# A hand-written attention schedule: a pair's loads and splits, the inverse rows and the branch fill moved to other slots

## The chip, the cores and the metric

One core of a Trainium2 chip runs the whole program. The metric is the device time of one execution in microseconds (us), the median of several runs. TensorE (PE) does the matmuls; VectorE (DVE) and ScalarE (ACT) read its results from PSUM; GpSimd (POOL) adds the mask; SyncE (SP) issues nearly all loads. Each of them takes its own instructions in the order of the program.

## The reference

One layer of an encoder, over 1024 positions of width 1024, all in float32:

```python
h = rmsnorm(x, norm_mix_pre)
m = mixer(h, w_in, b_f, conv_w, w_branch, w_out)
x = x + rmsnorm(m, norm_mix_post)
h = rmsnorm(x, norm_ffn_pre)
x = x + rmsnorm(swiglu(h, w_gate_up, w_down), norm_ffn_post)
```

The mixer has two branches. A is a gated short convolution, `ya`. B is causal softmax attention of 8 heads of width 64, whose logits carry a bias from cumulated forget gates, `yb`. They meet in

```python
merged = sigmoid(gate_conv) * (ya @ w_branch[0]) + sigmoid(gate_attn) * (yb @ w_branch[1])
return merged @ w_out
```

## The kernel before

Every product of two float32 operands is made of three: each operand is split into a rounded high part (a copy on ACT) and the rest (a subtraction on VectorE), and `mm3` multiplies high by high, high by low and low by high. The kernel projects q, k, v, the gates and the convolution's inputs, runs the attention, then the product with `w_branch[1]` (tile `pbb`), `w_out`, and the feed-forward part. The change touches the attention only, some 180 us of the span.

**Steps and slots.** Heads go in pairs `j` = 0 to 3 (the two heads are `e` = 0, 1), queries in blocks `i` of 128. A step (j, i) handles one query block of one pair against its (i + 1) * 128 keys. `steps` (line 697) lists the 32 steps: pairs 0 to 2 go from i = 7 down to 0, pair 3 goes 3, 2, 1, 0, 7, 6, 5, 4. A step is *wide* where its scores need over 512 columns. The loop at line 1008 runs slots t = 2 to 33; steps 0 and 1 are begun inside the projection before it (`last_pair`). In slot t stand, in this order of the program:

- `step_qk(t)`: the scores of step t, tiles `sp`. A wide step takes both score banks, a narrow one takes one; a bank is free again when the row maxima that read it are done.
- `pv_pair(t - 2)`: the products of the weights of step t - 2 with v, tile `po`, drained into `yb` on ACT every fourth step.
- `turn_bank(t - 1, ...)`: the exponentials of step t - 1 are transposed on PE (tiles `tps`, two banks) and copied to `ptT`, partly on ACT and partly on VectorE.
- `row_max(t, e)` on VectorE (a custom operation that adds the bias row `cb`, writes `pt` and leaves the negated maximum `nm`), then `expo(t, e)` on ACT, which also sums the rows into `rsum`.
- `mask_of(t + 1)` on POOL.
- `units[t]` units of *branch fill*: a unit is three matmuls (one k of an `mm3`) of `ya @ w_branch[0]`, tile `pba`, in bank `mb`. Four units make a half of one of eight column blocks `d`; then VectorE multiplies it by the gate into `um`. On PE the units stand between the transpositions of the two heads.
- whatever the table `at[t]` (lines 980 to 1006) lists for the slot.

The table's entries are `load_pair(j)` (bias rows `cb`, q and k, v), `split_q` and `split_k` (the quarter splits of q into `hi` and `lo`, and of k, whose low half is subtracted in place: tile `lo` or `kl`), `load_ya` and `split_ya` (`yh`, `yl`), `load_wa`, `split_wa` (`s`, `s4h`, `s4l`) and `load_sg` (gates), `load_wb` and `split_wb`, and the inverse rows: `invert(j)` takes the reciprocals `ri` of the row sums on VectorE, transposes them on PE (`tr`, in a `tps` bank), copies `tr` to `rT` on VectorE, stores that to memory (`ri_dram`) and loads it back spread over the partitions (`rb`). `divide(j, n)` multiplies half n of `yb` by `rb`.

Since the instructions of the attention are kept in the program's order (`strict`), an engine that waits holds back all that stands behind it in its queue. SyncE has nothing but loads and stores to do, and issues each as soon as its buffer and its data allow, often ahead of the slot that lists it.

**Where things stand.** Before the change `load_pair(j + 1)` is listed in slot 8j + 4, its splits in 8j + 5 to 8j + 7, so the last one, with the subtraction of the low half of k, right ahead of the pair's first slot 8j + 8. `invert(j)` stands at the end of slot 8j + 9, a wide step. Pair 3 is inverted in two halves, at the end of slot 29 and behind the loop. The fill covers d = 0 to 5 and ends in slot 31. Behind the loop `load_wa(7)` is issued, and four halves of branch products (d = 6, 7) run on the banks of `psm2`, beside the splits of `wb` and `yb`; then come the `pbb` products. All recorded instructions have line 73, that of a helper, so they are told apart by tiles.

Of the kernel before, what the change touches and what calls it, by code (L numbers as in the profile page):

```python
# [10 lines left out]
F32 = mybir.dt.float32  # L11
# [6 lines left out]
P = 128  # L18
S = 1024
D = 1024  # L20
KT = D // P
ST = S // P
NC = 512
H = 8
HD = 64
# [20 lines left out]
def block_kernel(  # L46
# [18 lines left out]
    class InOrder:  # L65
# [46 lines left out]
    def mul(o, a, b):  # L112
        nc.vector.tensor_tensor(o, a, b, op=ALU.mult)
# [53 lines left out]
    def st_tile(name, w=1):  # L167
        return stat.tile([P, w], F32, tag=name, name=name)
# [470 lines left out]
    def row_max(t, e):  # L639

        j, i = steps[t]
        n = (i + 1) * P
        sp, b = sps[t][e]
        cb = cb_of(j, e, j == 3 and i > 3)
        pt, nm = p_tile(t, e), st_tile("nm")
        if n <= NC:
            args = pt[:, :n], sp[:, b, :n], cb[:, :n]
        else:
            args = (
                pt[:, :n].rearrange("p (b k) -> p b k", b=2),  # L650
                sp[:, :, : n // 2],
                cb[:, :n].rearrange("p (b k) -> p b k", b=2),
            )
# [214 lines left out]
    def load_wa(d):  # L868
        was[d] = s4_t()
        nc.sync.dma_start(  # L870
            was[d], w_branch[0, 0][:, d * P : (d + 1) * P].rearrange("(k p) m -> p k m", p=P)
        )

    def load_sg(d):
        for n, ns in enumerate((n1, n2)):
            sgs[d, n] = sg_tile()
            nc.sync.dma_start(sgs[d, n], sg_dram[d][0][:, ns])

    def split_wa(d):
        wh, wl = s4h_t(), s4l_t()  # L880
        split(wh, wl, was[d])
        was[d] = wh, wl

    def branch_a(d, n, psp, tag):

        ns = (n1, n2)[n]
        ps = psp.tile([P, NC], F32, tag=tag, name="pba")
        wh, wl = was[d]
        for k in range(4):
            mm3(  # L890
                ps, (wh[:, k, :], wl[:, k, :]), (ya2[n][0][:, k, :], ya2[n][1][:, k, :]),
                k == 0, k == 3,
            )
            yield None if k < 3 else lambda: mul(um[:, d, ns], sgs[d, n], ps)

    FILL = 6

    def filler():
        for d in range(FILL):
            for n in range(2):  # L900
                yield from branch_a(d, n, pst, "mb")

    def inverse_rows(j, half=None):

        rs = rsums[j].rearrange("p (e i) -> p e i", e=2)
        if half is not None:
            rs = rs[:, :, 4 * half : 4 * half + 4]
        w = rs.shape[-1]
        ri = st_tile("ri", 2 * ST)[:, : 2 * w].rearrange("p (e i) -> p e i", e=2)
        nc.vector.reciprocal(ri, rs)  # L910
        tr = pss.tile([P, 4, P], F32, tag="T", name="tr", bufs=2)[: 2 * w, 0, :]
        nc.tensor.transpose(tr, ri.rearrange("p e i -> p (e i)"), ident)
        rT = t1.tile([2 * ST, P], F32, tag="rT", name="rT", bufs=2)[: 2 * w, :]
        nc.vector.tensor_copy(rT, tr)
        to = slice(0, S) if half is None else (n1, n2)[half]
        for e in range(2):
            nc.sync.dma_start(
                ri_dram[j][e][to].rearrange("(i p) -> i p", p=P), rT[e * w : (e + 1) * w, :]
            )
        rb = tp_.tile([P, S], F32, tag="rb", name="rb", bufs=1)[:, : w * P]  # L920
        for e in range(2):
            nc.sync.dma_start(
                rb[e * HD : (e + 1) * HD, :], ri_dram[j][e][to].partition_broadcast(HD)
            )
        return rb
# [22 lines left out]
    def divide(j, n, half=None):  # L948
        ns = (n1, n2)[n]
        mul(yb[:, j, ns], yb[:, j, ns], rbs[j][:, ns if half is None else n1])  # L950

    fill = filler()
    units = {t: 1 for t in (9, 10, *range(16, 20), *range(28, 32))}
    for t in (12, 20, 24):
        units |= {t - 1 if t == 12 else t: 2, t: 2, t + 1: 2, t + 2: 4, t + 3: 4}
    rbs, wbr = {}, {}
    wbh, wbl = [], []

    def invert(j, half=None):
        rbs[j] = inverse_rows(j, half)  # L960

    def load_pair(j):
        cb_of(j, 0)
# [13 lines left out]
    def do(f, *args):  # L977
        return lambda: f(*args)

    at = defaultdict(list)  # L980
    for j in range(3):
        o = 8 * j
        at[o + 4].append(do(load_pair, j + 1))
        at[o + 5] += [do(qk_tiles, j + 1), do(split_q, j + 1, n1)]
        at[o + 6] += [do(split_q, j + 1, n2), do(split_k, j + 1, n1)]
        at[o + 7].append(do(split_k, j + 1, n2))
        at[o + 9].append(do(invert, j))
        for n in range(2):
            at[o + 12 + n].append(do(divide, j, n))
    at[29].append(do(invert, 3, 0))  # L990
    at[32].append(do(divide, 3, 0, 0))
    at[25] += [do(cb_of, 3, 0, True), do(cb_of, 3, 1, True)]
    for t, n, m in ((2, 0, 0), (5, 0, 2), (9, 1, 0), (11, 1, 2)):
        at[t].append(do(load_ya, n, m))
    for t, n, m in (
        (3, 0, 0), (4, 0, 1), (7, 0, 2), (8, 0, 3), (10, 1, 0), (11, 1, 1), (12, 1, 2), (12, 1, 3),
    ):
        at[t].append(do(split_ya, n, m))
    for d, t in enumerate((5, 10, 13, 16, 21, 24, 26)):
        at[t] += [do(load_wa, d), do(load_sg, d)]  # L1000
    for d, t in enumerate((8, 11, 15, 19, 22, 25, 28)):
        at[t].append(do(split_wa, d))
    for k in range(4):
        at[26].append(do(load_wb, k))
# [1 line left out]
        at[t].append(do(split_wb, k))  # L1006

    for t in range(2, NU + 2):
        if t < NU:
            step_qk(t)  # L1010
        pv_pair(t - 2)
        back = t - 1 if t <= NU else None
        wide = back and steps[back][1] > 5
        if back:
            da = turn_bank(back, 0, 0, "ACT")
            db = turn_bank(back, 0, 1, "DVE")
            da()
        if t < NU:
            row_max(t, 0)
        if back and db:  # L1020
            db()
        if t < NU:
            expo(t, 0)
        muls = [m for m in (next(fill, None) for _ in range(units.get(t, 0))) if m]
        if back:
            dc = turn_bank(back, 1, 0, "ACT" if wide else "DVE")
            dd = turn_bank(back, 1, 1, "DVE" if wide else "ACT")
        if t < NU:
            row_max(t, 1)
# [12 lines left out]
    assert not at, at  # L1042
    invert(3, 1)
    for unit in fill:
        if unit:
            unit()
    pss_close()
    pst_close()

# [4 lines left out]
    def yb_split(n, ks):  # L1054
        ns = (n1, n2)[n]
        for k in ks:
            split(yb2[n][0][:, k, :], yb2[n][1][:, k, :], yb[:, k, ns])

    load_wa(KT - 1)
    for m in branch_a(KT - 2, 0, psm, "mm"):  # L1060
        pass
    m()
    split_wa(KT - 1)
    load_sg(KT - 1)
    split_wb(2)
    for m in branch_a(KT - 1, 0, psm, "mm"):
        pass
# [8 lines left out]
    m()  # L1076
    for m in branch_a(KT - 1, 1, psm, "mm"):
        pass
    yb_split(0, (2, 3))
    m()  # L1080
    divide(3, 1, 1)
    yb2.append(halves_of(1))
    yb_split(1, range(4))
    strict[0] = False
# [447 lines left out]
```

## Time and profile before

| what | value |
|---|---|
| median of 3 runs | 1395.58 us (1395.28 to 1396.58) |
| the profiled execution | 1396.29 us |
| its span, first to last instruction | 1394.5 us |
| PE busy | 1351.4 us (97%) |
| VectorE busy | 935.6 us (67%) |
| ACT busy | 536.4 us (38%) |
| mean granted clock of PE | 0.991 |

A row of the timeline gives the start in us from the span's start, the duration in us, engine, line, operation, `out<-in`, the shapes, the count, and in brackets the engine's idle time before it with what ended it. A row of the sums by stretch gives the stretch, its length, then for PE, PE's weight loads, VectorE, ACT and POOL the busy time with the number of instructions, the granted PE clock (1.00 is full, 0.50 half), and the DMA share with GB/s. Matmuls overlap in the records, so a row of 0.39 us may start 0.23 us after the one before. Slot t begins with its first `sp` row; slot 8 is at 445.06, slot 16 at 491.23, slot 24 at 533.63.

### The profile page before, as it was taken

How to read it: one execution, taken by the hardware profiler on the slowest of the kernel's cores; microseconds unless marked ns; L12 is line 12 of the kernel's file. 1: busy time of each engine (PE TensorE's matmuls, PEld its weight loads, DVE VectorE, ACT ScalarE, POOL GpSimd, SP SyncE). 2: the span in 40 equal slices, each digit the busy share in tenths (PEclk: the TensorE clock that was granted, in tenths of full speed). 3: DMA queues.
4: the chain of work that ended last, by engine and by line, in shares of the span. 5: the costliest groups of instructions: out<-in, count | busy, mean ns of one | idle time of the engine just before them, and what ended most of it. 6: DMA issues, size and time to landing. Idle time of an engine off the chain costs nothing.

```text
span 1394.5 us, 17740 instructions
## 1 busy us (share of the span) xinstructions
PE 1351.4 (97%) x6726; PEld 1102.9 (79%) x6726; DVE 935.6 (67%) x1451; ACT 536.4 (38%) x853; POOL 127.5 (9%) x256
## 2 busy tenths in 40 slices
PE   7999999999998999799999999999999999999997
PEld 7978888888876776688887778888888888888886
DVE  6873767655546654584678699767776676776585
ACT  6541222233345653442446432222232223444452
POOL 0001000011112111000001121111100111000000
PEclk9999999999999999999999999999999999999999
DMA  6332422333314543353234556332332325975541
GB/s 213 106 99 83 137 65 87 114 98 121 106 64 141 167 129 113 130 183 120 91 102 139 161 183 186 98 114 99 113 97 100 113 99 181 353 273 188 173 159 61
DMA packets 153558, 186.88 MB, mean 134 GB/s; under 512 B 9456, under 2 KB 106800, under 8 KB 153472
## 3 DMA queue, kind: packets, MB, share of 16 engines
q1 hardware_dynamic: 138736, 137.19, 31.4%
q0 software_dynamic: 14736, 48.54, 9.4%
q8 instruction: 53, 0.87, 0.2%
q14 instruction: 33, 0.27, 0.1%
HBM read 136.62 MB, written 49.09 MB: 133 GB/s over the span
## 4 chain that ended last, share of the span: by engine, by line
PE 54%; DVE 3%; issue 2%; ACT 1%; DMA 1%; POOL 0%; SPq 0%; DVEq 0%; POOLq 0%; ACTq 0%
PE b L73 27%; PE pd L73 15%; PE pm L73 5%; PE pbb L73 3%; PE pba L73 2%; PE po L73 1%; PE sp L73 0%; DVE tt L73 0%; PE tps L73 0%; PE tp L73 0%; DMA pre_dram<-c 0%; ACT tt L73 0%; ACT pt L73 0%; DVE ptT L73 0%; DMA raw<-in_w_gate_up_dram 0%
## 5 line engine op out<-in xcount | busy, mean ns | idle before, releaser
L73 DVE TENSOR_TENSOR c<-c,b 128x512 f32<-128x512 f32 x195 | 133.1, 683 | 95.8 <-PE b L73 76.8
L73 DVE TENSOR_TENSOR lo<-raw,hi 128x1024 fp32r<-128x1024 f32 (+1 forms) x93 | 112.1, 1205 | 86.0 <-PE b L73 71.4
L73 ACT ACTIVATE hi<-raw 128x1024 fp32r<-128x1024 f32 (+1 forms) x100 | 101.8, 1018 | 130.8 <-PE b L73 76.7
L73 PE MATMUL b<-hth,hi 128*128 128x512 f32 x352 | 139.0, 395 | 0.0
L73 PE MATMUL b<-hth,lo 128*128 128x512 f32 x352 | 138.1, 392 | 0.0
L73 PE MATMUL b<-htl,hi 128*128 128x512 f32 x352 | 137.2, 390 | 0.0
L73 ACT ACTIVATE hi<-sx 128x1024 fp32r<-128x1024 f32 x41 | 43.5, 1061 | 223.1 <-PE b L73 197.5
L73 PEld LDWEIGHTS b<-hth,lo 128*128 128x128 f32 x352 | 66.0, 188 | 15.6
L73 PEld LDWEIGHTS b<-hth,hi 128*128 128x128 f32 x352 | 66.1, 188 | 14.6 <-DVE c L73 0.8
L73 PEld LDWEIGHTS b<-htl,hi 128*128 128x128 f32 x352 | 66.1, 188 | 14.6
L73 DVE TENSOR_TENSOR lo<-sx,hi 128x1024 fp32r<-128x1024 f32 x41 | 50.2, 1224 | 34.4 <-PE b L73 30.8
L73 PE MATMUL b<-hah,hi 128*128 128x512 f32 x176 | 70.4, 403 | 1.9 <-ACT c L73 1.9
L73 PE MATMUL b<-hah,lo 128*128 128x512 f32 x176 | 69.5, 396 | 0.0
L73 PE MATMUL b<-hal,hi 128*128 128x512 f32 x176 | 69.3, 394 | 0.0
L73 DVE TENSOR_TENSOR sx<-raw 128x512 f32<-128x512 f32 x78 | 53.7, 688 | 20.4 <-DMA raw<-in_w_in_dram 10.8
L73 PE MATMUL pd<-hi,lo 128*128 128x512 f32 x160 | 62.6, 391 | 0.0
L73 PE MATMUL pd<-hi 128*128 128x512 f32 x160 | 62.3, 392 | 0.0
L73 PE MATMUL pd<-glo,ghi 128*128 128x512 f32 x148 | 57.7, 390 | 0.0
L73 PE MATMUL pd<-ghi 128*128 128x512 f32 x148 | 57.6, 390 | 0.0
L73 PE MATMUL pd<-ghi,glo 128*128 128x512 f32 x148 | 57.6, 389 | 0.0
L73 PE MATMUL b<-hT34h,lo 128*128 128x512 f32 x136 | 53.4, 393 | 0.0
L73 PE MATMUL b<-hT12h,lo 128*128 128x512 f32 x136 | 53.4, 393 | 0.0
(364 smaller groups left out, 3401.2 us busy)
## 6 DMA issues: line engine op xcount, KB each, us to landing
raw<-in_w_gate_up_dram SPq DMA_DIRECT2D x51, 512.0 KB, 3.7
raw<-in_w_in_dram SPq DMA_DIRECT2D x35, 512.0 KB, 4.5
a_dramS<-um POOLq DMA_DIRECT2D x44, 256.0 KB, 2.8
a_dramA<-um POOLq DMA_DIRECT2D x33, 256.0 KB, 2.8
xt<-in_x_dram SPq DMA_DIRECT2D x16, 512.0 KB, 3.5
sg<-sg_dram SPq DMA_DIRECT2D x32, 256.0 KB, 4.3
graw<-a_dramS SPq DMA_DIRECT2D x14, 512.0 KB
sg_dram<-c POOLq DMA_DIRECT2D x24, 256.0 KB, 2.3
```

The costliest lines, as they stand in the source:

```text
L73: ins = getattr(self.engine, name)(*args, **kw)
```

## The change

It rewrites the slot table and three pieces of code around it.

- `load_pair(j + 1)` moves from slot 8j + 4 to 8j + 2, the quarter splits from 8j + 5 to 7 to 8j + 4 to 6. The loads and splits of `ya`, of the branch weights and of the gates get new slots; d = 7 is now loaded and split inside the loop.
- The inverse is cut in two. `inverse(j)`, the reciprocal, stands at the end of slot 8j + 10. `inverse_rows` stands in slot 8j + 12, a narrow step (for pair 2 that is slot 28, a wide one): the transposition right behind the scores, in the branch bank `mb`, and `rT` behind the slot's first row maximum. The divisions move two slots on. Pair 3 is inverted once, not in halves, at the end of slot 32 and in slot 33.
- The fill begins in slot 8, covers 13 halves instead of 12 (d = 6, n = 0 is the new one), and has units in slots 32 and 33.
- In slots 2 to 7 the first head's transpositions stand ahead of `pv_pair`, not behind it.

The core of the diff:

```diff
-        at[o + 4].append(do(load_pair, j + 1))
-        at[o + 5] += [do(qk_tiles, j + 1), do(split_q, j + 1, n1)]
-        at[o + 6] += [do(split_q, j + 1, n2), do(split_k, j + 1, n1)]
-        at[o + 7].append(do(split_k, j + 1, n2))
-        at[o + 9].append(do(invert, j))
+        at[o + 2].append(do(load_pair, j + 1))
+        at[o + 4] += [do(qk_tiles, j + 1), do(split_q, j + 1, n1)]
+        at[o + 5] += [do(split_q, j + 1, n2), do(split_k, j + 1, n1)]
+        at[o + 6].append(do(split_k, j + 1, n2))
+        at[o + 10].append(do(inverse, j))
+        rows[o + 12] = j
         for n in range(2):
-            at[o + 12 + n].append(do(divide, j, n))
-    at[29].append(do(invert, 3, 0))
-    at[32].append(do(divide, 3, 0, 0))
+            at[o + 14 + n].append(do(divide, j, n))
+    at[32].append(do(inverse, 3))
...
-    for d, t in enumerate((8, 11, 15, 19, 22, 25, 28)):
+    for d, t in enumerate((7, 11, 15, 18, 22, 25, 28, 32)):
         at[t].append(do(split_wa, d))
...
     for t in range(2, NU + 2):
+        turned = None
         if t < NU:
             step_qk(t)
-        pv_pair(t - 2)
+        if t in rows:
+            turned = inverse_rows(rows[t], pst, "mb")
+        if t == NU + 1:
+            turned = inverse_rows(3, pss, "T", 2)
...
+        if t >= 8:
+            pv_pair(t - 2)
         if back:
             da = turn_bank(back, 0, 0, "ACT")
             db = turn_bank(back, 0, 1, "DVE")
             da()
+        if t < 8:
+            pv_pair(t - 2)
         if t < NU:
             row_max(t, 0)
+        if turned:
+            turned()
...
-    invert(3, 1)
-    for unit in fill:
-        if unit:
-            unit()
...
-    load_wa(KT - 1)
-    for m in branch_a(KT - 2, 0, psm, "mm"):
-        pass
-    m()
-    split_wa(KT - 1)
-    load_sg(KT - 1)
...
+    divide(3, 0)
     yb_split(0, (2, 3))
     m()
-    divide(3, 1, 1)
+    divide(3, 1)
```

In the new `units` the slots 8 to 15 have 1, 1, 1, 1, 2, 2, 4, 4 units (before, from slot 9: 1, 1, 2, 2, 2, 4, 4), slots 16 to 31 what they had, slots 32 and 33 two each.

VectorE, from the last drain of slot 6 to the first row maximum of slot 8 (`ISA pt,nm` is a row maximum, `ISA nm` its read-out). Before:

```order
L73 COPY ptT<-tps 128x384
L73 SCALAR_TENSOR_TENSOR lo<-raw,hi 128x512
L73 ISA pt,nm<-sp,cb 128x128
L73 ISA nm 128x1
L73 ISA pt,nm<-sp,cb 128x128
L73 ISA nm 128x1
L73 COPY ptT<-tps 128x256
L73 TENSOR_TENSOR lo<-lo,hi 128x1024
L73 TENSOR_TENSOR yl_3476<-raw,yh_3475 128x512
L73 ISA pt,nm<-sp,cb 128x1024
```

and now:

```order
L73 COPY ptT<-tps 128x384
L73 TENSOR_TENSOR lo<-lo,hi 128x1024
L73 TENSOR_TENSOR yl_3476<-raw,yh_3475 128x512
L73 ISA pt,nm<-sp,cb 128x128
L73 ISA nm 128x1
L73 ISA pt,nm<-sp,cb 128x128
L73 ISA nm 128x1
L73 COPY ptT<-tps 128x256
L73 TENSOR_TENSOR yl_3476<-raw,yh_3475 128x512
L73 TENSOR_TENSOR s4l<-s_3684,s4h 128x512
L73 ISA pt,nm<-sp,cb 128x1024
```

The subtraction of the low half of k (`lo<-lo,hi`) and a `yl` have moved ahead of slot 7's two row maxima; another `yl` and the weight split `s4l` now stand behind them.

PE, at the inverse rows of pair 0. Before, `tr` is the first matmul behind slot 9's transpositions, ahead of slot 10's scores:

```order
L73 MATMUL tps<-ident,pt 128x128 x8
L73 MATMUL tr<-ident,ri 16x128
L73 MATMUL sp<-hi 128x384 x2
L73 MATMUL sp<-lo,hi 128x384 x2
L73 MATMUL sp<-hi,lo 128x384 x2
```

Now it stands in slot 12, between the scores and the value products:

```order
L73 MATMUL sp<-hi 128x512 x2
L73 MATMUL sp<-lo,hi 128x512 x2
L73 MATMUL sp<-hi,lo 128x512 x2
L73 MATMUL tr<-ident,ri 16x128
L73 MATMUL po<-ptT,v 64x128 x12
L73 MATMUL tps<-ident,pt 128x128 x5
```

It has moved from behind a pair of transpositions to behind a step's scores, with the value products queued behind it.

PE, slots 32 and 33. Before:

```order
L73 MATMUL po<-ptT,v 64x128 x12
L73 MATMUL tps<-ident,pt 128x128 x10
L73 MATMUL po<-ptT,v 64x128 x10
L73 MATMUL tr<-ident,ri 8x128
L73 MATMUL pba<-yh_3475,s4h 128x512
```

and now:

```order
L73 MATMUL po<-ptT,v 64x128 x12
L73 MATMUL tps<-ident,pt 128x128 x5
L73 MATMUL pba<-yh_3475,s4h 128x512
L73 MATMUL pba<-yl_3476,s4h 128x512
L73 MATMUL pba<-yh_3475,s4l 128x512
L73 MATMUL pba<-yh_3475,s4h 128x512
L73 MATMUL pba<-yl_3476,s4h 128x512
L73 MATMUL pba<-yh_3475,s4l 128x512
L73 MATMUL tps<-ident,pt 128x128 x5
L73 MATMUL tr<-ident,ri 16x128
L73 MATMUL po<-ptT,v 64x128 x10
L73 MATMUL pba<-yh_3475,s4h 128x512
```

Six branch products have come between the two heads' transpositions, and `tr` stands ahead of the last value products.

More of the change, by code (lines that the diff above doesn't have):

```diff
@@ L894, in branch_a, with inverse, inverse_rows, drain @@
             yield None if k < 3 else lambda: mul(um[:, d, ns], sgs[d, n], ps)
-    FILL = 6
+    FILL = 2 * 6 + 1
     def filler():
[L899 to L925, printed above, removed]
+        for h in range(FILL):
+            yield from branch_a(h // 2, h % 2, pst, "mb")
+    invs, rbs = {}, {}
+    def inverse(j):
+        invs[j] = st_tile("ri", 2 * ST)
+        nc.vector.reciprocal(invs[j], rsums[j])
+    def inverse_rows(j, psp, tag, bufs=1):
+        tr = psp.tile([P, 4, P], F32, tag=tag, name="tr", bufs=bufs)[: 2 * ST, 0, :]
+        nc.tensor.transpose(tr, invs[j], ident)
+        def drain():
+            rT = t1.tile([2 * ST, P], F32, tag="rT", name="rT", bufs=2)
+            nc.vector.tensor_copy(rT, tr)
+            for e in range(2):
+                nc.sync.dma_start(
+                    ri_dram[j][e].rearrange("(i p) -> i p", p=P), rT[e * ST : (e + 1) * ST, :]
+                )
+            rb = rbs[j] = tp_.tile([P, S], F32, tag="rb", name="rb", bufs=1)
+            for e in range(2):
+                nc.sync.dma_start(
+                    rb[e * HD : (e + 1) * HD, :], ri_dram[j][e].partition_broadcast(HD)
+                )
+        return drain
     po = [None]
@@ L946, in pv_pair, with divide @@
             )
-    def divide(j, n, half=None):
+    def divide(j, n):
         ns = (n1, n2)[n]
-        mul(yb[:, j, ns], yb[:, j, ns], rbs[j][:, ns if half is None else n1])
+        mul(yb[:, j, ns], yb[:, j, ns], rbs[j][:, ns])
     fill = filler()
[L953 to L956, printed above, removed]
+    units = {}
+    for t in range(8, 32, 8):
+        if t < 24:
+            units |= {t: 1, t + 1: 1, t + 2: 1, t + 3: 1, t + 4: 2, t + 5: 2, t + 6: 4, t + 7: 4}
+        else:
+            units |= {t: 2, t + 1: 2, t + 2: 4, t + 3: 4, t + 4: 1, t + 5: 1, t + 6: 1, t + 7: 1}
+    units |= {32: 2, 33: 2}
+    wbr = {}
     wbh, wbl = [], []
-    def invert(j, half=None):
-        rbs[j] = inverse_rows(j, half)
     def load_pair(j):
@@ L978, in do @@
         return lambda: f(*args)
-    at = defaultdict(list)
+    at, rows = defaultdict(list), {}
+    at[2].append(do(load_ya, 0, 0))
     for j in range(3):
         o = 8 * j
-        at[o + 4].append(do(load_pair, j + 1))
-        at[o + 5] += [do(qk_tiles, j + 1), do(split_q, j + 1, n1)]
-        at[o + 6] += [do(split_q, j + 1, n2), do(split_k, j + 1, n1)]
-        at[o + 7].append(do(split_k, j + 1, n2))
-        at[o + 9].append(do(invert, j))
+        at[o + 2].append(do(load_pair, j + 1))
[4 more added lines that the diff above has]
+        rows[o + 12] = j
         for n in range(2):
-            at[o + 12 + n].append(do(divide, j, n))
-    at[29].append(do(invert, 3, 0))
-    at[32].append(do(divide, 3, 0, 0))
+            at[o + 14 + n].append(do(divide, j, n))
+    at[32].append(do(inverse, 3))
     at[25] += [do(cb_of, 3, 0, True), do(cb_of, 3, 1, True)]
-    for t, n, m in ((2, 0, 0), (5, 0, 2), (9, 1, 0), (11, 1, 2)):
+    for t, n, m in ((3, 0, 2), (3, 1, 0), (6, 1, 2)):
         at[t].append(do(load_ya, n, m))
     for t, n, m in (
-        (3, 0, 0), (4, 0, 1), (7, 0, 2), (8, 0, 3), (10, 1, 0), (11, 1, 1), (12, 1, 2), (12, 1, 3),
+        (3, 0, 0), (4, 0, 1), (6, 0, 2), (7, 0, 3), (8, 1, 0), (9, 1, 1), (10, 1, 2), (11, 1, 3),
     ):
         at[t].append(do(split_ya, n, m))
-    for d, t in enumerate((5, 10, 13, 16, 21, 24, 26)):
-        at[t] += [do(load_wa, d), do(load_sg, d)]
-    for d, t in enumerate((8, 11, 15, 19, 22, 25, 28)):
+    for d, t in enumerate((4, 8, 12, 15, 19, 23, 26, 29)):
+        at[t].append(do(load_wa, d))
+    for d, t in enumerate((4, 8, 14, 16, 22, 24, 27, 32)):
+        at[t].append(do(load_sg, d))
+    for d, t in enumerate((7, 11, 15, 18, 22, 25, 28, 32)):
         at[t].append(do(split_wa, d))
@@ L1041, in block_kernel @@
             f()
-    assert not at, at
-    invert(3, 1)
-    for unit in fill:
-        if unit:
-            unit()
+    assert not at and next(fill, None) is None, at
     pss_close()
```

## The prediction

> **What bounds the kernel now.** The page first. TensorE (PE) is busy nearly all the span:
>
> ```profile
> PE 1351.4 (97%) x6726; PEld 1102.9 (79%) x6726; DVE 935.6 (67%) x1451; ACT 536.4 (38%) x853; POOL 127.5 (9%) x256
> ```
>
> The profiled execution took 1396.29 us, 0.71 over the median 1395.58; the sum below is a difference, and I take it off the median. An edit that moves work can only win PE's waits or its clock. So the view of waits comes second, for PE alone between 420 and 620 us, the stretch of the attention loop:
>
> ```profile
> PE tr L73 <- DVE ri L73: 5.7, 4, 1.8
> PE sp L73 <- DVE lo L73: 3.9, 2, 2.0
> PE pba L73 <- ACT s4h L73: 3.3, 1, 3.3
> PE sp L73 <- DVE kl L73: 1.8, 1, 1.8
> PE sp L73 <- DVE nm L73: 1.7, 3, 0.6
> PE tps L73 <- DVE ptT L73: 1.6, 3, 0.7
> PE po L73 <- DVE ptT L73: 1.1, 3, 0.4
> PE tps L73 <- ACT ptT L73: 0.8, 2, 0.5
> PE pba L73 <- ACT yb L73: 0.5, 1, 0.5
> ```
>
> Columns: us in total, times, longest. Together 20.4 us. The third view is the sums by stretch, whose column before the last two is the granted clock. Four stretches hold half-clock time: slot 8 (445.06), slot 24 (533.63), slot 30 (567.03) and the branch products behind the loop (586.20). The others are slots 11, 16, 18, 19 and 26, for comparison:
>
> ```profile
> 445.06:452.04 6.98, 4.80 (x23) 2.72 (x22) 4.08 (x11) 2.22 (x7) 0.04 (x1) 0.76 0.01 4
> 465.76:471.47 5.71, 5.71 (x59) 4.87 (x59) 2.97 (x8) 3.34 (x7) 0.92 (x2) 1.00 0.96 312
> 491.23:496.56 5.33, 3.51 (x26) 2.16 (x26) 4.21 (x7) 0.41 (x2) 0.14 (x1) 1.00 0.23 69
> 503.26:508.78 5.52, 5.52 (x63) 4.74 (x62) 2.60 (x6) 1.75 (x6) 0.46 (x1) 1.00 0.48 119
> 508.78:513.88 5.10, 5.10 (x56) 4.26 (x55) 2.74 (x9) 2.69 (x6) 0.97 (x3) 1.00 0.99 314
> 533.63:540.38 6.75, 4.93 (x24) 3.06 (x23) 3.47 (x7) 1.68 (x5) 0.92 (x2) 0.76 0.19 66
> 545.87:551.05 5.18, 5.18 (x41) 4.13 (x41) 1.57 (x6) 1.47 (x5) 0.87 (x2) 1.00 0.51 112
> 567.03:574.15 7.12, 7.12 (x62) 6.14 (x61) 3.77 (x7) 2.14 (x5) 0.45 (x1) 0.76 0.51 148
> 586.20:604.00 17.80, 14.51 (x49) 11.26 (x50) 7.55 (x11) 7.19 (x11) 0.00 (x0) 0.81 0.41 132
> ```
>
> So waits and clock together offer about 28 us, and no edit here can win more.
>
> **1. Loads and quarter splits.** The loads gain nothing by themselves: SyncE runs ahead of the slots as buffers come free, and pair 1's rows, placed in slot 4, were issued at slot 2's end:
>
> ```profile
> 425.99 0.91 SPq L73 DMA_DIRECT2D cb<-c_dram x2
> 446.94 1.23 DVE L73 TENSOR_TENSOR lo<-lo,hi 128x1024 fp32r<-128x1024 f32 x1 [0.98 <-ACT hi L73]
> 448.08 0.68 DVE L73 TENSOR_TENSOR yl<-raw,yh 128x512 fp32r<-128x512 f32 x1
> 444.52 0.69 DVE L73 SCALAR_TENSOR_TENSOR lo<-raw,hi 128x512 fp32r<-128x512 f32 x1 [0.93 <-ACT hi L73]
> ```
>
> The splits do. The next pair's scores stop for the low half of k (`lo`, `kl`): 2.0, 1.9 and 1.8 us. One slot earlier that subtraction is over before slots 16 and 24 ask, under 12 branch products each in slots 14, 15, 22 and 23. In slot 16 a division and the weight split, about 0.7 each, still stand ahead of the row maximum; I give 0.3 back there: 1.5 and 1.8. The first pair has no branch fill above it. There 1.23 + 0.68 now stand on VectorE before slot 7's row maxima in place of 0.69, so those end 1.1 to 1.2 later, and they free the bank that slot 8's second head needs. Against 2.0 lost I expect 1.6 again: 0.4. Sum 3.7; bounds 2.5 (first gone wholly, second 1.0) to 5.5.
>
> **2. Half clock.** Cost: one minus the granted clock, times the stretch: 0.24 x 6.98 = 1.7 (slot 8, of which PE would in part have waited for row maxima: 1.1), 0.24 x 6.75 = 1.6 (slot 24, 1.45 with the wait in it), 0.19 x 17.8 = 3.4 (behind the loop, 2.8 while it had work). Slot 30 against slot 18, which does the same work at full clock: 7.12 - 5.52 = 1.6, of which 0.5 returns, as row maximum and copies are then last. Each stretch follows a PE wait of 1.7 us or more, and those waits go. Sum 6.4; bounds 3.0 (two stretches return) to 7.4. [...]
>
> **3. Inverse rows.** Before, PE's transposition of the reciprocals (`tr`) stands first in a slot, behind copy and reciprocal:
>
> ```profile
> 460.01 0.27 PE L73 MATMUL tr<-ident,ri 128*16 128x128 f32 x1 [1.20 <-DVE ri L73]
> 503.06 0.27 PE L73 MATMUL tr<-ident,ri 128*16 128x128 f32 x1 [1.07 <-DVE ri L73]
> 545.67 0.27 PE L73 MATMUL tr<-ident,ri 128*16 128x128 f32 x1 [1.63 <-DVE ri L73]
> 566.83 0.27 PE L73 MATMUL tr<-ident,ri 128*8 128x128 f32 x1 [1.75 <-DVE ri L73]
> 459.01 0.08 DVE L73 DVE_READ_ACCUMULATOR2_ANT nm<- 128x1 f32 x1
> 502.07 0.08 DVE L73 DVE_READ_ACCUMULATOR2_ANT nm<- 128x1 f32 x1
> 565.29 0.08 DVE L73 DVE_READ_ACCUMULATOR2_ANT nm<- 128x1 f32 x1
> 503.26 0.44 PE L73 MATMUL sp<-hi 64*128 64x384 f32 x2
> ```
>
> The scores follow 0.20 after (503.26 - 503.06). Without `tr` three of the four sites still wait for the second row maximum, read out at 459.09, 502.15 and 565.37. They start earlier by 460.21 - 459.09 = 1.1, 1.1 and 567.03 - 565.37 = 1.65; the narrow one, at 545.67, by 1.63 + 0.20 = 1.8. Sum 5.65.
>
> The new place costs. In slots 12 and 20 `tr` writes the branch bank, so PE waits for the product just finished to be drained, with the value products (`po`) queued behind:
>
> ```profile
> 472.15 0.68 DVE L73 TENSOR_TENSOR um<-sg,pba 128x512 f32<-128x512 f32 x1
> 472.37 1.53 PE L73 MATMUL po<-ptT,v 128*64 128x128 f32 x24
> 474.59 0.68 DVE L73 CUSTOM_DVE_ANT_0 pt<-sp,cb 128x512 f32<-128x512 f32 x1
> ```
>
> `um` ends at 472.83, `po` stood ready at 472.37: 0.5 and 0.2 for `tr`, twice 0.7. In slot 12 the next branch product must also wait until `rT` is copied, behind the row maximum at 474.59: 0.4 more. In slot 28 the row maxima are last anyway: 0.2. Net 5.65 - 2.0 = 3.6; bounds 2.0 to 5.2.
>
> **4. Slots 2 to 7.** `po` now stands between the two heads' transpositions and covers their drains:
>
> ```profile
> 436.00 0.74 PE L73 MATMUL tps<-ident,pt 128*128 128x128 f32 x5 [0.48 <-DVE ptT L73]
> 443.64 0.87 PE L73 MATMUL po<-ptT,v 128*64 128x128 f32 x10 [0.30 <-DVE ptT L73]
> ```
>
> With the 0.8 on ACT's `ptT` that is 1.6. In slots 5 to 7 the first head's transposition comes before its exponential is ready; I give 0.7 back: 0.9; bounds 0 to 1.6.
>
> **5. Slot 32 and the tail.** Two units of branch fill stand in slot 32 between the transpositions, two in slot 33, and d = 7's weights are loaded and split inside the loop.
>
> ```profile
> 582.82 0.74 PE L73 MATMUL tps<-ident,pt 128*128 128x128 f32 x5 [0.48 <-DVE ptT L73]
> 584.23 1.31 PE L73 MATMUL po<-ptT,v 128*64 128x128 f32 x18 [0.31 <-DVE ptT L73]
> 588.43 0.58 SPq L73 DMA_DIRECT2D s<-in_w_branch_dram x1
> 591.85 0.63 ACT L73 ACTIVATE s4h<-s 128x512 fp32r<-128x512 f32 x1 [5.68 <-DMA s<-in_w_branch_dram]
> ```
>
> Gone: 3.3 (`s4h`), 0.5 (`yb`), 0.5 and 0.3. New: `tr` of the last pair stands before `po`, behind copy and reciprocal as at 503.06, so about 0.95 + 0.2. The last pair's whole division now comes behind a round trip through memory, but 42 branch products lie above it, 8.5 us at the 0.2 apiece that three more of them make in slot 11 than in slot 19 (5.71 - 5.10). Net 3.4; bounds 2.0 to 4.5. Products and DMAs keep their number but for one transposition, two `ri` stores and two `rb` loads; POOL's masks stay.
>
> **6. One unit from slot 11 to slot 8.** Slot 8 waits for row maxima anyway; slot 11 falls from 5.71 to slot 19's 5.10: 0.6; bounds 0 to 0.6.
>
> Sum: 3.7 + 6.4 + 3.6 + 0.9 + 3.4 + 0.6 = 18.6. 1395.6 - 18.6 = 1377.0.
>
> **The rivals.** *Waits that move.* VectorE and ACT work their queues in order, so the earlier splits hold back row maxima in slots 7 to 10, PE's new waits again pass 1.7 us, and half clock returns there and in one later slot. Then terms 1 and 2 stand at their lower ends (2.5 and 3.0), 3 and 4 lose 1.5: 18.6 - 1.2 - 3.4 - 1.5 = 12.5, so 1383. For it: the 1.6 of part 1 lies close to the 1.7. *The clock does not follow these waits.* In slot 16 a wait of 1.8, and before slot 26 one of 1.63, left the clock at 1.00, so the windows could fall where they will: term 2 is 0, 1383.4. [...] Against it: four of four half-clock stretches stand right behind such waits. *Nothing moves.* The loads already ran ahead, and if row maxima are last wherever a wait goes, 1395. Against it: PE's transpositions end long before the row maxima only at the wide steps. *Branch weights arrive late: slower.* ACT stops in order for them. At 591.85 it stood 5.7 us, and PE 3.3, with 3.4 from issue (588.43) to use. If each of seven loads inside the loop brought such a stop, 7 x 3.3 = 23 us against 18.6: 1400. It decides once a load lands over one slot late; against it, the table gives each two to three slots of some 5 us.
>
> **How the numbers follow.** Forecast 0.66; moved waits 0.17; clock 0.05; nothing 0.03; late weights 0.04; better than all my terms but within the 28 us 0.05. Lower end: the upper bounds, 5.5 + 7.4 + 5.2 + 1.6 + 4.5 + 0.6 = 24.8, give 1371. Upper end: the lower bounds, 2.5 + 3.0 + 2.0 + 0 + 2.0 + 0 = 9.5, would give 1386; that they meet is unlikely, and 1384.5 takes in both rivals near 1383. About 0.15 lies outside. By 0.2% (2.8 us, about what a measurement of this kernel can tell from no change): faster 0.93, same 0.03, slower 0.04.
>
> **What would show it.** Right: no PE wait on `lo`, `kl`, `s4h` or, at slots 9, 17, 25 and 29, on `ri`; one wait on `ri` near 1 us before the last `po`; waits on `nm` in their place of 0.1 to 0.6; a wait of `tr` on `um` near 0.5 twice; granted clock 1.00 in slots 24 and 30 and in the tail; the stretch from slot 2 to the first `pbb` some 18 us shorter. Wrong: half clock in two or more stretches, waits over 1 us on `nm` or `ptT` in slots 7 to 10, ACT stopped for `in_w_branch`, or a wait in the `pbb` products for the last division.

## The result, and the profile after

The changed kernel takes 1373.8 us (1373.32 to 1374.06, 4 runs) against 1395.43 for the kernel before on the same chip: a ratio of 0.9847, 95% interval 0.983 to 0.9864. It is 21.6 us faster; 18.6 were forecast. The profiled execution took 1373.6 us, with a span of 1371.8. PE's row of the page, and PE's waits between 420 and 620 us (us in total, times, longest):

```profile
PE 1341.8 (98%) x6725; PEld 1096.7 (80%) x6725; DVE 933.8 (68%) x1449; ACT 536.1 (39%) x853; POOL 127.9 (9%) x256
```

```profile
PE sp L73 <- DVE nm L73: 3.3, 5, 1.2
PE pba L73 <- DVE rT L73: 1.1, 2, 0.7
PE tps L73 <- ACT pt L73: 1.0, 2, 0.6
PE tr L73 <- ACT s4h L73: 0.9, 1, 0.9
PE tr L73 <- DVE um L73: 0.5, 2, 0.3
PE po L73 <- DVE ptT L73: 0.4, 1, 0.4
PE tps L73 <- DVE ptT L73: 0.2, 1, 0.2
```

The waits on `lo`, `kl`, `ri` and `s4h` that stood at the head of the list are gone, 20.4 us have become 7.4. (The row that names `s4h` is the last pair's `tr`, which waits for its reciprocal. In the variant below that has no weight split there, a_tail_back, the same wait of 0.9 stands as `tr <- DVE ri`.) The sums by stretch place the gain: a stretch runs from one slot's first scores to another's, the last one to the first `pbb`. Of the kernel before, as far as the prediction has not shown them:

```profile
421.85:445.06 23.21, 21.60 (x236) 17.05 (x235) 13.74 (x33) 15.72 (x38) 5.90 (x13) 1.00 0.59 204
452.04:460.21 8.17, 5.61 (x38) 3.73 (x38) 5.90 (x12) 7.17 (x14) 1.78 (x4) 1.00 0.00 0
460.21:491.23 31.02, 31.02 (x280) 25.23 (x280) 18.54 (x45) 18.62 (x46) 5.37 (x12) 1.00 0.57 188
496.56:503.26 6.70, 5.12 (x37) 3.78 (x36) 4.68 (x10) 5.98 (x11) 1.68 (x4) 1.00 0.18 62
503.26:533.63 30.37, 30.37 (x278) 24.57 (x278) 16.86 (x42) 16.27 (x42) 5.38 (x12) 1.00 0.47 143
540.38:545.87 5.49, 3.86 (x26) 2.78 (x25) 2.78 (x8) 2.91 (x7) 0.93 (x2) 0.98 0.00 0
545.87:559.20 13.33, 13.33 (x101) 10.17 (x100) 5.50 (x17) 2.97 (x12) 1.82 (x5) 1.00 0.80 255
559.20:567.03 7.83, 5.33 (x37) 3.74 (x36) 6.75 (x13) 7.20 (x13) 1.79 (x4) 1.00 0.35 140
574.15:603.77 29.62, 24.64 (x160) 19.19 (x159) 14.37 (x26) 13.57 (x23) 0.46 (x1) 0.88 0.32 106
```

and of the changed one:

```profile
422.27:444.14 21.87, 20.91 (x235) 16.42 (x234) 14.12 (x34) 16.73 (x40) 5.92 (x13) 1.00 0.76 265
444.14:449.65 5.51, 3.82 (x26) 2.34 (x26) 4.53 (x12) 2.41 (x8) 0.00 (x0) 1.00 0.03 7
449.65:455.57 5.92, 5.08 (x35) 3.67 (x35) 4.24 (x8) 5.25 (x10) 1.37 (x3) 1.00 0.93 244
455.57:487.58 32.01, 31.35 (x279) 24.88 (x278) 19.69 (x48) 19.20 (x46) 5.87 (x13) 1.00 0.33 104
487.58:491.11 3.53, 3.31 (x27) 2.16 (x26) 3.42 (x7) 0.28 (x1) 0.00 (x0) 1.00 0.02 5
491.11:496.63 5.52, 4.84 (x35) 3.67 (x35) 3.85 (x7) 4.82 (x9) 1.37 (x3) 1.00 0.77 217
496.63:527.83 31.20, 30.93 (x278) 24.84 (x277) 18.40 (x46) 17.45 (x43) 5.88 (x13) 1.00 0.35 116
527.83:531.07 3.24, 3.24 (x23) 2.15 (x22) 2.84 (x7) 1.08 (x4) 0.67 (x2) 1.00 0.75 234
531.07:534.58 3.51, 3.51 (x25) 2.61 (x25) 1.34 (x5) 2.98 (x9) 1.17 (x3) 1.00 0.74 297
534.58:549.32 14.74, 14.07 (x101) 10.49 (x100) 7.74 (x20) 4.75 (x16) 2.18 (x5) 1.00 0.60 198
549.32:554.18 4.86, 4.81 (x36) 3.72 (x35) 3.32 (x8) 4.14 (x9) 0.92 (x2) 1.00 0.64 171
554.18:560.12 5.94, 5.94 (x62) 4.91 (x61) 4.34 (x9) 4.17 (x8) 0.93 (x2) 1.00 0.25 76
560.12:582.48 22.36, 21.00 (x159) 17.07 (x159) 15.13 (x28) 13.46 (x23) 0.46 (x1) 1.00 0.49 151
```

| slots | before | after | won | forecast, from its parts |
|---|---|---|---|---|
| 2 to 7 | 23.21 | 21.87 | 1.3 | 0.9 (4) |
| 8 | 6.98 | 5.51 | 1.5 | 1.5 (1, 2) |
| 9 | 8.17 | 5.92 | 2.3 | 1.1 (3) |
| 10 to 15 | 31.02 | 32.01 | -1.0 | -0.5 (3, 6) |
| 16 | 5.33 | 3.53 | 1.8 | 1.5 (1) |
| 17 | 6.70 | 5.52 | 1.2 | 1.1 (3) |
| 18 to 23 | 30.37 | 31.20 | -0.8 | -0.7 (3) |
| 24 | 6.75 | 3.24 | 3.5 | 3.25 (1, 2) |
| 25 | 5.49 | 3.51 | 2.0 | 1.8 (3) |
| 26 to 29 | 21.16 | 19.60 | 1.6 | 1.45 (3) |
| 30 | 7.12 | 5.94 | 1.2 | 1.1 (2) |
| 31 to the first `pbb` | 29.62 | 22.36 | 7.3 | 6.2 (2, 5) |
| sum | 181.92 | 160.21 | 21.7 | 18.7 (18.6 before rounding) |

The two spans differ by 22.7: 21.7 here, 0.4 lost ahead of slot 2, and 1.4 won behind the first `pbb`, a part that the change doesn't touch (below). The granted clock, 0.76 to 0.88 in four of the stretches before, is 1.00 in all in this profile; a second one, below, shows half clock in slot 8.

### The profile page after: what moved, and what is told of

Same layout as the page of the kernel before. It is cut to its first block, busy times and chain, and to the rows that moved or that the text cites. A ratio compares the mean times of both kernels' runs of the same rounds, so it can differ in the third digit from the quotient of the medians.

```text
span 1371.8 us, 17726 instructions
## 1 busy us (share of the span) xinstructions
PE 1341.8 (98%) x6725; PEld 1096.7 (80%) x6725; DVE 933.8 (68%) x1449; ACT 536.1 (39%) x853; POOL 127.9 (9%) x256
## 4 chain that ended last, share of the span: by engine, by line
PE 86%; DVE 5%; ACT 3%; DMA 3%; issue 2%; POOL 0%; DVEq 0%; ACTq 0%; POOLq 0%
PE b L73 52%; PE pd L73 15%; PE pm L73 5%; PE pbb L73 3%; PE pba L73 3%; PE po L73 2%; PE tps L73 2%; PE sp L73 2%; DVE t L73 1%; ACT pt L73 1%; DVE pt L73 1%; PE pv L73 1%; PE ma L73 1%; DMA pre_dram<-s 1%; PE tp L73 1%
```

## Experiments

Each is an edit of the changed kernel, but for one of the kernel before. Where a variant is compared with the changed kernel, the latter's 1374.48 from the first group is taken (1395.02 for the kernel before there). The kernel before gave medians of 1394.36 to 1395.43 in the four groups, single runs from 1390.45 to 1398.37; the four medians lie 1.1 apart, so a difference under about 1 between groups says little.

**The changed kernel again.**

> The changed kernel itself, beside its variants on one chip. Every theory: 1373.8 within 0.5, no half clock in the attention loop or the tail. If the half clock only happened to fall elsewhere in the one profile (windows free-running, blind to the waits), some executions should show it, and the times should spread over 3 us as those of the kernel before do (1392.98 to 1396.58).

1374.48 us (1372.71 to 1375.76), ratio 0.9853 (0.9839 to 0.9867). The time came back, 0.2 over what I allowed, but half clock came too, and the runs spread over 3.05: the two signs that I had named for a clock blind to the waits. What the clock went with is worked out under the next two runs. In the profile before, half clock begins at 448.44, 537.18, 567.90 and 591.80, which lie 26, 9 and 7 times 3.413 us apart, and lasts 3.41 or twice that. Carried on as a grid, this divides a profile into windows of 3.41 us. Here are the window that ends at 445.90 and the next, in this profile, then the like place in the first profile of the changed kernel:

```profile
442.48:445.90 3.42, 2.18 (x21) 1.22 (x17) 2.49 (x6) 2.24 (x7) 1.52 (x4) 1.00 0.13 48
445.90:449.31 3.41, 3.04 (x13) 2.02 (x15) 2.35 (x8) 1.92 (x6) 0.00 (x0) 0.50 0.02 5
```

```profile
443.19:446.60 3.41, 2.16 (x21) 1.41 (x19) 2.58 (x7) 2.03 (x8) 0.45 (x2) 1.00 0.04 14
446.60:450.01 3.41, 2.97 (x23) 1.73 (x19) 2.85 (x5) 1.64 (x5) 0.34 (x1) 1.00 0.09 24
```

The same slot 8, with the same wait of 1.25, fell to half clock in one execution, for two windows (449.31:452.72 is at 0.50 too), and not in the other: slot 8 lies 0.37 later here, and the grid 0.7 earlier. (The busy times, 2.18 and 2.16, hardly differ, as records of matmuls overlap; the shares below do.) It cost 0.8: slots 2 to `pbb` took 160.99 against 160.21.

**Half clock: one long wait, or two short ones.** VectorE was given work on a tile `dm` of its own.

```diff
+        stall(stalls.get(t, 0))     # c_one: {9:3, 12:4, 16:3, 19:4, 24:3, 28:4, 30:3}
         if t < NU:
             row_max(t, 0)
...
+        stall(stalls2.get(t, 0))    # c_two: 1 or 2 ahead of head 0, 1 ahead of head 1
         if t < NU:
             row_max(t, 1)
```

> The changed kernel with idle work added on VectorE: 3 or 4 products of 128x512 on a tile that nothing else uses (0.69 each) ahead of the first row maximum of slots 9, 12, 16, 19, 24, 28 and 30, to make PE wait once for 1 to 3 us at each place. Waits alone: 24 x 0.69 = 16.5 less the slack of each place, about 12: 1386. Theory (half clock in the window of 3.41 us behind every window in which PE streams under half of the time): some 4 to 6 half-clock windows, each right behind such a window and behind no other, 1.5 us apiece: about 1393. Rival, the clock falls only behind a window with no matmul in it at all, or blind to waits: granted clock 1.00 at these places, 1386.

> The changed kernel with the same kind of idle work cut in two: 1 or 2 products ahead of the first and 1 ahead of the second row maximum of slots 8, 12, 16, 19, 24, 28 and 30, so that PE waits twice for about 1 us with matmuls between, each wait under 1.7. Waits alone: 19 x 0.69 = 13 less slack, about 8: 1382. Theory (PE's streamed share of a window decides, so waits add up): half clock behind two or more of the windows that hold both waits, about 1385. Rival (one wait of over 1.7 is needed): no half clock, 1382, but for slot 8, where it already comes and goes.

c_one took 1393.87 us, with half clock behind four windows of the attention (one of them slot 8's, which has no added work; the profile's granted clock over its span is 0.990), close to the 1393 of the theory. c_two took 1388.95, with half clock behind two. A window of c_two with the one behind it, and the rows of PE's waits in it:

```profile
450.98:454.39 3.41, 1.08 (x6) 0.44 (x6) 3.41 (x7) 1.34 (x3) 0.96 (x2) 1.00 0.67 208
454.39:457.80 3.41, 3.41 (x18) 2.40 (x19) 1.71 (x4) 2.02 (x4) 0.34 (x1) 0.50 0.67 183
```

```profile
452.50 0.47 PE L73 MATMUL sp<-hi 64*128 64x448 f32 x1 [1.05 <-DVE nm L73]
454.25 0.63 PE L73 MATMUL sp<-hi 64*128 64x448 f32 x1 [1.28 <-DVE nm L73]
```

No wait there reaches 1.7; the two come to 2.33 of the window's 3.41, and 0.50 follows all the same. For all 14 profiles I worked out how much of each window of the grid PE streamed. A matmul of 512 columns starts 0.23 us after the one before and is recorded for 0.39 (`pba` at 582.02 and 582.25 in the changed kernel), so 0.16 was taken off each record, transpositions included. Among windows that start between 20 and 1360 us and are themselves at full clock, 40 have a share under one half, and 30 of these were followed by half clock (all 9 under 0.3, 10 of 12 from 0.3 to 0.4, 11 of 19 from 0.4 to 0.5); of 5409 at or above one half, one was, at 0.507. (The profile before has 5 of 6 and none of 381, the first of the changed kernel none of 2 and none of 390.) In these profiles half clock thus came behind a share under one half in all cases counted but one, and the more often the lower the share.

Slot 8 stands as in the changed kernel in eight of the profiles (both of the changed kernel, and a_inverse_back, a_tail_back, a_pv_back, a_loads_late, a_loads_3 and c_one). The window there has a share of 0.47 to 0.51 in six, and all six fell; it has 0.52 and 0.53 in the other two, a_pv_back and the first profile of the changed kernel, and neither fell.

The rival by which one wait of over 1.7 is needed falls. So does that of c_one, by which the window must hold no matmul: 450.98:454.39 had 1.08 us of matmul in it, 442.48:445.90 had 2.18, and 0.50 followed both. c_two was 4 slower than I put it, and not for its waits: from slot 2 to `pbb` they come to 14.8 against the changed kernel's 7.4, so 7.4 more where I expected 8. PE's busy time grew by 5.1, with three windows at half clock, and a fourth lies at 72 us, ahead of the attention.

**The splits one slot later again.**

```diff
-        at[o + 4] += [do(qk_tiles, j + 1), do(split_q, j + 1, n1)]
-        at[o + 5] += [do(split_q, j + 1, n2), do(split_k, j + 1, n1)]
-        at[o + 6].append(do(split_k, j + 1, n2))
+        at[o + 5] += [do(qk_tiles, j + 1), do(split_q, j + 1, n1)]
+        at[o + 6] += [do(split_q, j + 1, n2), do(split_k, j + 1, n1)]
+        at[o + 7].append(do(split_k, j + 1, n2))
```

> The changed kernel with the quarter splits of the next pair one slot later again (slots o+5, o+6, o+7), loads and everything else as changed. Theory (PE waits for the low half of k, and half clock follows a wait that leaves PE under half busy in a window of 3.41 us): waits on lo or kl of about 2 us before slots 8, 16 and 24 come back, 3.7 us, and half clock in slots 8 and 24, 2.5 us: about 1380.0. Rival, clock blind to the waits: 1377.5, granted clock 1.00 in both slots. Rival, the earlier loads did it: no change, 1373.8.

1383.34 us (1381.9 to 1386.23): 8.9 slower, 6.2 expected. The loads stood early in this run, so it tells the splits from the loads. PE's waits:

```profile
PE sp L73 <- DVE lo L73: 4.5, 2, 2.4
PE sp L73 <- DVE kl L73: 2.4, 1, 2.4
```

That is 6.9 against 5.7 before, and half clock came back in slots 8, 24 and now also 16 (behind 533.30:536.71, with 1.68 us of PE in it, and 492.34:495.75, with 1.37; 0.990 over the span).

**The inverse rows back behind slot o + 9** (pairs 0 to 2; whole inverse at the end of the slot, `tr` in a `tps` bank; the step is wide for pairs 0 and 1, and narrow for pair 2).

```diff
-        at[o + 10].append(do(inverse, j))
-        rows[o + 12] = j
+        at[o + 9] += [do(inverse, j), do(rows_now, j)]   # inverse_rows(j, pss, "T", 2)()
```

> The changed kernel with the reciprocals and their transposition back in one piece behind slots 9, 17 and 25, in the bank of the transpositions, for pairs 0 to 2; the last pair stays as changed. Theory: the transposition again stands first in slots 10, 18 and 26, about 1.0, 1.0 and 1.5 us behind the reciprocal, 0.2 each for itself and what follows; the waits of it on um (0.5 in all) and of pba on rT (1.1) go: +2.5, about 1376.3, and no half clock, as each wait is under 1.7. Rival, the row maxima are last there anyway: within 0.5 of 1373.8. Rival, clock follows smaller waits too: half clock in slot 26, 1378.

1377.2 us (1376.69 to 1379.26): 2.7 slower, between the 1376.3 of the theory and the 1378 of the rival. PE's waits:

```profile
PE tr L73 <- DVE ri L73: 3.9, 3, 1.6
```

Half clock did come in slot 26 (0.996 over the span), as the rival had it; I had ruled it out for waits under 1.7. So the 2.7 is not the waits alone.

**The tail's weights back behind the loop.**

```diff
-    units |= {32: 2, 33: 2}
...
+    load_wa(KT - 1)                 # and FILL = 12, no load or split of d = 7 in the table
+    for m in branch_a(KT - 2, 0, psm, "mm"):
+        pass
+    m()
+    split_wa(KT - 1)
+    load_sg(KT - 1)
```

> The changed kernel with the last branch weights (d = 7) loaded and split behind the loop again and no branch products in slots 32 and 33; the last pair's inverse in one piece stays. Theory: ACT stands for the weights, PE waits about 3.3 us on s4h, waits of 0.5 and 0.3 come back in slots 32 and 33, and two windows at half clock follow, 2.8: about 1380.7. Rival, clock blind to the waits: 1377.9. Rival, the 12 products that now stand behind the loop cover the load: 1374.5.

1382.14 us (1381.89 to 1383.34): 7.7 slower, 1.4 over what was expected. The stretch from slot 31 to the first `pbb` is 29.66 again, as before the change. PE's wait is back, and two windows at half clock behind it (575.40:578.82 has 1.39 us of PE, 578.82:582.23 is at 0.50):

```profile
PE pba L73 <- ACT s4h L73: 2.9, 1, 2.9
```

**The value products first in slots 2 to 7 again** (`pv_pair(t - 2)` ahead of `turn_bank` for every t).

> The changed kernel with the value products ahead of the transpositions in slots 2 to 7 too, as before. Theory: waits of tps and po on ptT of 1.6 in all come back, and those of tps on pt in slots 6 and 7 (0.95) go: +0.7, 1374.8; if the row maximum of slot 8 comes earlier by it, nothing. Rival (the order is worth its full 1.6): 1375.7.

1377.02 us (1376.19 to 1378.29): 2.5 slower. The profile has a half-clock window at 71 us, far ahead of the attention (0.998 over the span), so the whole time is no clean measure; slots 2 to 7 alone took 447.28 - 423.83 = 23.45 against 21.87, so the order is worth 1.6, the rival's value.

**Part 1 alone, on the kernel before** (loads in o + 2, splits in o + 4 to o + 6; the first load of `ya` is listed ahead of them in slot 2).

> The kernel before with part 1 of the change alone: the next pair's rows are loaded from slot o+2 and split in slots o+4, o+5 and o+6. Theory: PE's waits on lo and kl (5.8 in all) go except for the row maxima that are then last before slot 8, and the half clock of slots 8 and 24 goes, that of slot 30 and of the tail stays: 1395.0 - 6.2 = 1388.8 by the terms of the prediction. If part 1 is worth as much alone as taking it out of the changed kernel cost (9.2), 1385.8. Rival, clock blind to the waits: 1391.3.

1392.71 us against 1394.36, ratio 0.9985 (0.9973 to 0.9997): a quarter of what was expected. The waits on `lo` and `kl` are gone, and a new one has come. SyncE's queue, then ACT and PE:

```profile
464.49 0.61 SPq L73 DMA_DIRECT2D v<-v_dram  x1
465.20 3.10 SPq L73 DMA_DIRECT2D s<-in_w_branch_dram  x1
```

```profile
475.98 0.63 ACT L73 ACTIVATE s4h<-s 128x512 fp32r<-128x512 f32 x1 [4.54 <-DMA s<-in_w_branch_dram]
```

```profile
477.15 1.53 PE L73 MATMUL tps<-ident,pt 128*128 128x128 f32 x5 [3.08 <-ACT ptT L73]
```

In the old table the branch weights `s` of slot 10 now queue behind pair 2's loads (before, they were issued at 464.24, ahead of those). ACT stops 4.5 us for them, the copies of the transpositions that PE waits for stand behind it, and two windows of half clock follow (0.995 over the span). That is the rival "branch weights arrive late". ACT has no such stop in the changed kernel, where `load_wa` has new slots; that these are what keeps it out was not tried alone.

**The loads of pairs 2 and 3 later, the early splits kept.**

```diff
-        at[o + 2].append(do(load_pair, j + 1))
+        at[o + (4 if j else 2)].append(do(load_pair, j + 1))   # a_loads_3: 3 in place of 4
```

> The changed kernel with the loads of pairs 2 and 3 back in slots 12 and 20 (the slot in which their first split stands), all else as changed. Theory (SyncE runs ahead, so the loads' place in the table gains nothing): 1374.1 within 0.5, no wait of ACT on the loaded rows. Rival (the loads had to come two slots earlier for the early splits): each load of 4 us stands ahead of the split, ACT and then PE stop about 3 us in slots 12 to 14 and 20 to 22: 1380.

> The changed kernel with the loads of pairs 2 and 3 in slots 11 and 19: one slot later than changed and one earlier than in the run that lost 18 us with them in slots 12 and 20. Theory (what counts is whether SyncE's queue has them ahead of or behind the store of the inverse rows, which waits for the transposition in slot 12 or 20): they are still ahead of it, issue within 1 us of the changed kernel's 449.94, no stop of ACT: 1374.1 within 0.5. Rival (the splits need the loads two whole slots ahead, in proportion): about half of the loss, 1383.

In slots 12 and 20: 1392.69 us, ratio 0.9981 (0.997 to 0.9992). Nearly the whole gain is lost; I had forecast no change, and the rival a third of this loss. In slots 11 and 19: 1375.57, ratio 0.9868 (0.9848 to 0.9889). That is 1.1 over the changed kernel, but the intervals overlap, and from slot 2 to `pbb` this profile took 160.99, as the second one of the changed kernel. SyncE's queue with the loads in slot 12, and what ACT and PE then wait for:

```profile
471.12 0.65 SPq L73 DMA_DIRECT2D ri_dram<-rT  x2
...
474.71 0.42 SPq L73 DMA_DIRECT2D raw<-qk_dram  x1
```

```profile
ACT hi L73 <- DMA raw<-qk_dram: 16.8, 2, 8.6
```

```profile
484.31 0.69 PE L73 MATMUL po<-ptT,v 128*64 128x128 f32 x2 [6.00 <-ACT ptT L73]
```

PE waits so twice, 12.3 us in all, and three and two windows of half clock follow (at 480.45 and 531.65; 0.992 over the span). And with them in slot 11:

```profile
450.65 0.42 SPq L73 DMA_DIRECT2D raw<-qk_dram  x1
...
471.18 0.67 SPq L73 DMA_DIRECT2D ri_dram<-rT  x2
```

One slot in the table is 24 us at the queue. In both runs SyncE issues in the order of its list, and the store of the inverse rows, `ri_dram<-rT`, waits for the copy of slot 12's `tr`, until 471.12 and 471.18; ahead of it the loads of `raw` go out at 450.65, behind it at 474.71.

**Two places moved further.** i_order splits the first branch rows in slots 8 to 12 and puts the last `tr` behind the last `po`; i_more also copies `rT` ahead of the first row maximum and splits d = 2 in slot 14.

```diff
-        (3, 0, 0), (4, 0, 1), (6, 0, 2), (7, 0, 3), (8, 1, 0), (9, 1, 1), (10, 1, 2), (11, 1, 3),
+        (3, 0, 0), (4, 0, 1), (8, 0, 2), (9, 0, 3), (10, 1, 0), (11, 1, 1), (12, 1, 2), (12, 1, 3),
...
+        if turned:                  # i_more: moved up, with split_wa(2) in slot 14
+            turned()
         if t < NU:
             row_max(t, 0)
```

> The changed kernel with two places of its table moved on: the splits of the first branch rows as late as their products allow (slots 8 to 12 in place of 6 to 11), so that two subtractions less stand ahead of the row maxima of slots 7 and 8; and the last transposition of reciprocals behind the last value products. Theory: the waits of 1.25 in slot 8 and 0.92 in slot 33 go, and with the first the half clock that some executions show there: 1372.3 or less in every execution, spread under 1.5. Rival (the subtractions are only late one slot on): slot 9 waits for the row maximum by 1 us more, within 0.5 of 1374.1, only the 0.9 of slot 33 is won.

> As the run before, and the turned reciprocals copied ahead of the first row maximum in slots 12, 20 and 28, and the third weight split in slot 14 in place of 15. Theory: the waits of pba on rT (0.4 and 0.7) and of the scores on nm in slot 17 (0.9) shrink by 1 in all against that run: 1371.3. Rival (the copy then holds up row maxima, which are last in slots 13 and 29): no gain over it, or a loss of 0.5.

i_order 1372.92 us (1372.39 to 1373.78), ratio 0.9847 (0.983 to 0.9863); i_more 1371.26 (1370.3 to 1372.6), ratio 0.9835 (0.9818 to 0.9852). Slots 2 to `pbb` took 159.01 and 157.94 against 160.21, slot 8 of i_more 4.38 against 5.51, with no half clock in the attention in either profile (0.998 and 0.999 over the span). So both stretches go the expected way. But i_order's times lie up to 1.5 over the 1372.3 that I had put as its upper end, and against the changed kernel's 0.9853 (0.9839 to 0.9867) both intervals overlap: neither gain is shown by the times alone.

## Why the prediction held

Forecast 1377.0, range 1371 to 1384.5, measured 1373.8. Taken out one by one, the splits, the inverse rows of pairs 0 to 2, the tail and the order cost 8.9, 2.7, 7.7 and 1.6, 20.9 in all, beside the 20.5 that the whole won in the first group. So most of the gain comes from them. That the two sums meet is partly luck: the last pair's inverse, part 6 and the moved weight splits were not undone, so the four costs must overlap in part. Two bounds do not follow from the terms beside them: the full costs of half clock add up to 8.3, not 7.4, and part 1 at its lower end to 0 + 1.0 + 1.8 = 2.8, not 2.5. They would move the ends of the range by less than 1 us.

1. **Loads and splits.** Right in kind. Slots 8, 16 and 24 won 6.8, with their clock, against 6.25, in the profile in which slot 8 kept full clock. The new wait of slot 8 was 1.25, not 1.6:

```profile
445.89 0.50 PE L73 MATMUL sp<-hi 64*128 64x512 f32 x1 [1.25 <-DVE nm L73]
```

"The loads gain nothing by themselves" is the step that failed. It holds between slots 10 and 11, and fails at slot 12. It was read from the old table, in which the store of the inverse rows is listed in slot 9, three slots ahead of the loads. With the store moved to slot 12, a load listed in slot 12 goes out behind it and costs 18.2 us. I looked at what the loads moved past, and not at what was moved in front of them.

2. **Half clock.** All four stretches are at 1.00 in the profile of the result, and slots 24 and 30 and the tail won what was forecast or more. Putting the waits back brought half clock back in slot 24 and in the tail, so there the cause is shown; for slot 30 nothing was undone. What the term went by, "a PE wait of 1.7 us or more", was a stand-in: in the 14 profiles half clock went with PE's share of a window of 3.41 us, and 1.7 of one wait is half of that when it falls inside one. Of the waits that the prediction puts against itself, the 1.8 was divided between 489.40:492.81 and 492.81:496.22, with shares of 0.61 and 0.73, and the 1.63 left 0.44 in 544.01:547.42, one of the 10 of 40 behind which the clock stayed at 1.00. A wait of 1.25 stood ahead of 0.50 in slot 8.

In slot 8 the term was luck. Half clock came back there in six of the eight profiles that have this slot, at a cost of 0.8 in all where it was measured, of the 1.1 that the prediction counts for it. By this the rival "the clock does not follow these waits" is refuted as to the cause, but right in that the windows lie elsewhere from one execution to the next (one ends at 445.90 in the second profile of the changed kernel, at 446.60 in the first).

The 1.4 behind the first `pbb` is not the change's. A window before, 762.46:765.88, had 1.57 us of matmul and was followed by half clock; the like one now, 770.87:774.28, had 1.73 and was not. How much of the 1.4 this makes is not shown: among the profiles without half clock there, the part behind `pbb` takes 788.67 to 790.27.

3. **Inverse rows.** The new costs stand where forecast: `tr` behind `um` 0.5 in all, `pba` behind `rT` 0.40 in slot 12, and 0.67, not 0.2, in slot 28.

The gain was under-sized in slot 9: 2.3 against 1.1. Two things were left out. The weight split `s4l` stood ahead of the slot's first row maximum; it is now listed in slot 7 and done before slot 8's. These are VectorE's last instruction ahead of that row maximum, and the row maximum, before:

```profile
455.80 0.68 DVE L73 TENSOR_TENSOR s4l<-s,s4h 128x512 fp32r<-128x512 f32 x1
456.40 1.08 DVE L73 CUSTOM_DVE_ANT_0 pt<-sp,cb 128x896 f32<-128x896 f32 x1
```

and now:

```profile
452.63 0.69 DVE L73 TENSOR_TENSOR yl<-sx,yh 128x512 fp32r<-128x512 f32 x1 [1.68 <-ACT yh L73]
453.24 1.08 DVE L73 CUSTOM_DVE_ANT_0 pt<-sp,cb 128x896 f32<-128x896 f32 x1
```

Counted from the slot's first scores, the row maximum starts at 4.36 before and at 3.59 now, 0.77 earlier. And I held that the next scores would still wait for the second row maximum: slots 10, 18 and 30 begin without a wait, slot 10 at 455.57, with the second row maximum ending at 455.85. How the 2.3 divides is not shown, as the split was not moved back alone. With the inverse put back, slots 8 and 9 together took 13.31, against 12.23 in the second profile of the changed kernel, so it is worth some 1.1 there (slot 8 is at half clock in both, for one window and for two). The other sites came within 0.25.

4. **Slots 2 to 7.** 1.3 in the profile, 1.6 by the undoing, the upper bound: giving 0.7 back was too careful. The first head's transpositions did wait 0.95, in slots 6 and 7, but slots 5 to 7 together lost only 0.4 and slots 2 to 4 won 1.7; why so little was lost is not shown.

5. **The tail.** 7.3 with its clock against 6.2, all of it undone by moving the weights back (29.66 against 29.62 before). The new `tr` of slot 33 waited 0.92, as forecast:

```profile
571.17 0.27 PE L73 MATMUL tr<-ident,ri 128*16 128x128 f32 x1 [0.92 <-ACT s4h L73]
```

6. **The unit of slot 11.** Slots 10 to 15 lost 1.0 where -0.5 was forecast, so here no term can be told from another.

Of the rivals, "waits that move" came true in part: the largest moved wait is 1.25 and not 1.7, yet it brings half clock in slot 8 in most of the profiles. Late weights came only in the old table with part 1 alone.

## What to carry to other kernels

Give a step that others wait for a slot with filler above it, and then follow every queue that it and the steps around it pass through: here a store that waited for slot 12's `tr` held the loads listed behind it back until 474.71, where they went out at 450.65 ahead of it, and that one slot in the table, from 11 to 12, was worth 17 us. Price PE's waits by window, not one by one: here short waits that together left PE under half busy in 3.41 us (1.05 and 1.28 in c_two) cost their own length, and half clock came behind 30 of the 40 windows under half busy. Undo parts one at a time from the finished kernel as well as adding them to the old one: the early splits were worth 8.9 us in the new table, and loads and splits together 1.7 in the old.

## What the runs showed of the hardware

In the 14 profiles the granted clock fell to 0.50 for whole windows of 3.413 us (448.44:451.85 in the profile before, 445.90:452.72 in the second of the changed kernel), on a grid that lay elsewhere in each of these two. Of the windows counted in which PE streamed under half of the time, 30 of 40 were followed by it; of 5409 others, one was. A wait of 1.25 us beside narrow matmuls was enough in six profiles of eight (slot 8: half clock at shares of 0.47 to 0.51, none at 0.52 and 0.53). So near one half the same kernel showed both, which may be one source of the 8 us over which single runs of the kernel before are spread (1390.45, at 0.996 over the span, to 1398.37, at 0.989).
